# A hybrid layer's first stage: an earlier conditioning block, and two query units accumulated pair by pair

## The chip, the cores and the metric

The kernel runs on one core of a Trainium2 chip. The metric is the device time of one execution in microseconds (us), as the median of several runs. The engines are named as in the profile: PE is TensorE (PEld its weight loads), DVE is VectorE, ACT is ScalarE, POOL is GpSimd, and SP is SyncE, which here issues nearly all DMAs. TensorE's clock is granted at one of two levels, 1.2 and 2.4 GHz; the profile writes the granted share of the higher one.

## The reference

One layer of a diffusion backbone over 1024 tokens of width 1024, with 256 context tokens in front. What matters here is its beginning:

```python
mod = (jax.nn.silu(c) @ ada_w + ada_b)[:, None, :]
sh1, sc1, g1, sh2, sc2, g2 = jnp.split(mod, 6, axis=-1)
h = modulate(rms_norm(x, norm1_w), sh1, sc1)      # h * (1 + scale) + shift
p = h @ w_in                                      # queries, keys, values, z, and the SSD inputs
```

Neighbourhood attention and a bidirectional state-space scan then run on `p`, and an output projection, a second modulated norm and a gated MLP follow; a final norm ends the layer. All data are float32, and the products are computed from a high and a low part of each operand.

## The kernel before

Features lie on the 128 partitions. x is held as 8 feature tiles (`kt` 0 to 7) by 1024 tokens, in two halves of 512 tokens (`h` 0 and 1). A product of float32 accuracy is three matmuls: `hh` times `wh`, `hl` times `wh`, `hh` times `wl`, where `hh` and `hl` are the high and low part of the normalised input and `wh` and `wl` those of a weight block (`load_w`, L72 to L80, splits a loaded block `ws` on ACT and DVE). `mm3` (L82 to L89) runs these three over the feature tiles; a matmul takes 512 columns, so that 1024 tokens need two.

The conditioning (`ada`, L155 to L170) is done in eight blocks of 1 MB for the part that the first norm needs. Blocks 0 to 3 give the shift, blocks 4 to 7 the scale, two feature tiles each. A block is loaded into one of four buffers (`adaw`), multiplied on PE in 16 matmuls (`adap`), copied by ACT (`adas`), folded on PE (`mp`, 4 matmuls), and DVE adds the bias (`mod`, `modc`). The PSUM pool `m1p`, which `adap`, `mp` and the statistics share, has two slots.

The first stage (L129 to L200) loads x, forms for each half the sum of squares (`sq_x`, `sqa_x`), turns it by PE into a row of reciprocal roots (`stat_x`, `rst_x`, `dg_x`, and the broadcast `rbt`), and then goes over four pairs of feature tiles: blocks 4 + i and i of the conditioning, then for both halves and both tiles of the pair DVE's `ny`, ACT's `hh` and DVE's `hl` (`norm`, L172 to L176). Three weight blocks for the first query and key units are loaded on the way (`pre`). The PSUM pool `mmp` has three slots of 1024 columns: the broadcast rows hold one until the last `ny`, the query units take the others. The second stage (from L228) uses the memory that the first stage's pools have given back: it loads tables, the context tokens and 32 rows of the later conditioning (`adal`, L203 to L208), multiplies the two query and two key groups (`fu_qk`, 48 matmuls per unit), rotates them on DVE and stores them, and then computes the values (`tu_v`).

The order of the instructions on each engine and of the loads on SP is not the order of the program text. A planner simulates the program and lets each engine take, of what is ready by the simulated time, what stands first in the text; it also places the semaphore waits. On the chip every engine then keeps the planned order.

Of the kernel before, what the change touches and what calls it, by code (L numbers as in the profile page):

```python
# [10 lines left out]
FP = mybir.dt.float32  # L11
# [6 lines left out]
P = 128  # L18
T = 1024
TC = 256  # L20
KT = 8
# [15 lines left out]
def hymba(ctx: ExitStack, tc: tile.TileContext, A):  # L37
# [35 lines left out]
    def load_w(src, nk, nf, name):  # L73
        n = nk * nf
        s, h, l = (w_tile(tag, f"{tag}_{name}") for tag in ("ws", "wh", "wl"))
        sp.dma_start(s[:, :n], src)
        act.activation(h[:, :n], s[:, :n], AF.Copy)  # L77
        dve.tensor_tensor(l[:, :n], s[:, :n], f32(h[:, :n]), OP.subtract)
        pat = "p (k f) -> p k f"
        return h[:, :n].rearrange(pat, k=nk), l[:, :n].rearrange(pat, k=nk)  # L80
# [22 lines left out]
            pe.matmul(rb[:, t * P:e * P], ones, dg[:, t:e], start=True, stop=True)  # L103
        return rb

    # ---------------------------------------------------------------- projections
    pa = ExitStack()
    hx = pa.enter_context(tc.tile_pool(name="hx", reuse_waits="tile", bufs=1))
    pc = ExitStack()
# [8 lines left out]
    pre = {}  # L118

    with ExitStack() as p0:  # L120
        adap = p0.enter_context(tc.tile_pool(name="adap", reuse_waits="tile", bufs=4))
        xin = p0.enter_context(tc.tile_pool(name="xin", reuse_waits="tile", bufs=1))
        wk0 = p0.enter_context(tc.tile_pool(name="wk0", reuse_waits="tile", bufs=2))

        cc = wk0.tile([P, KT, 2], FP, name="cc", bufs=1)
        sc = hx.tile([P, KT, 32], FP, name="sc")
        sel = wk0.tile([P, 2], FP, name="sel", bufs=1)
        xt = xin.tile([P, KT, T], FP, name="xt")
        sp.dma_start(cc, A["cc"])  # L129
        xh = [xt[:, :, 512 * h:512 * h + 512] for h in range(2)]  # L130

        def load_x(h):
            for kt in range(0, KT, 2):
                sp.dma_start(xh[h][:, kt:kt + 2], A["xt"][:, kt:kt + 2, 512 * h:512 * h + 512])

        load_x(0)
        sp.dma_start(sel, A["sel"])
        sp.dma_start(vec, A["vec"])
        sp.dma_start(cst, A["cst"])
        dve.memset(sc, 0.0)  # L140
        act.activation(sc[:, :, 0:2], cc, AF.Silu)

        def stats(wk0, src, n, key):
            st = m1p.tile([P, 8], FP, tag="m1", name=f"stat_{key}")
            acc = wk0.tile([P, n * P], FP, tag=f"sqa{n}", name=f"sqa_{key}", bufs=1)
            for kt in range(KT):
                sq = acc if kt == 0 else wk0.tile([P, n * P], FP, tag=f"ny{n}", name=f"sq_{key}{kt}", bufs=n)
                act.activation(sq, src[:, kt], AF.Square)
                if kt:
                    dve.tensor_tensor(acc, acc, sq, OP.add)  # L150
            for t in range(n):
                pe.matmul(st[:, t:t + 1], acc[:, t * P:(t + 1) * P], ones1, start=True, stop=True)
            return st[:, :n]

        def ada(b):  # L155
            w = adap.tile([P, KT, 256], FP, tag="ada", name=f"adaw{b}")
            sp.dma_start(w, A["ada_w"][b])
            pr = m1p.tile([P, 256], FP, tag="m1", name=f"adap{b}")
            for kt in range(KT):
                j = kt % 4  # L160
                pe.matmul(pr[32 * j:32 * j + 32], sc[:, kt], w[:, kt], start=kt < 4, stop=kt >= 4,
                          skip_group_check=True)
            sb = wk0.tile([P, 256], FP, tag="adas", name=f"adas{b}")
            act.activation(sb, pr, AF.Copy)
            mp = m1p.tile([P, 2, 2], FP, tag="m1", name=f"mp{b}")
            for f in range(2):
                pe.matmul(mp[:, f], sb[:, f * P:(f + 1) * P], sel, start=True, stop=True)
            c0 = 2 * b
            for m_, col in ((mod, 0), (modc, 1)):
                dve.tensor_tensor(m_[:, c0:c0 + 2], mp[:, :, col], vec[:, V_AB + c0:V_AB + c0 + 2], OP.add)  # L170

        def norm(src, rb, a, b, oh, ol, kt, n, key):  # L172
            y = wk0.tile([P, n], FP, tag=f"ny{n // P}", name=f"ny_{key}{kt}", bufs=n // P)
            dve.scalar_tensor_tensor(y, src[:, kt], a, rb, OP.mult, OP.mult)
            act.activation(oh[:, kt], y, AF.Identity, bias=b)
            dve.scalar_tensor_tensor(ol[:, kt], y, b, f32(oh[:, kt]), OP.add, OP.subtract)  # L176

        rbt = mmp.tile([P, T], FP, tag="mm", name="rbt")
        rbx = [rbt[:, 512 * h:512 * h + 512] for h in range(2)]
        rstd_rows(mmp, wk0, stats(wk0, xh[0], 4, "x0"), 4, "mm", "x0", "sqa4", rb=rbx[0])  # L180
        for i in range(4):
            ada(4 + i)
            if i == 0:
                load_x(1)
            ada(i)
            if i < 3:
                pre[i] = load_w(A["wf"][8 + i], KT, P, f"qk0{i}")
            s2 = slice(2 * i, 2 * i + 2)
            for j, m_ in enumerate((mod, modc)):
                dve.scalar_tensor_tensor(scl[:, j, s2], m_[:, 8 + 2 * i:10 + 2 * i], 1.0,  # L190
                                         vec[:, V_N1 + 2 * i:V_N1 + 2 * i + 2], OP.add, OP.mult)
            for h in range(2):
                if i == 0 and h:
                    rstd_rows(mmp, wk0, stats(wk0, xh[1], 4, "x1"), 4, "mm", "x1", "sqa4", rb=rbx[1])
                for kt in (2 * i, 2 * i + 1):
                    c = slice(512 * h, 512 * h + 512)
                    norm(xh[h], rbx[h], scl[:, 0, kt:kt + 1], mod[:, kt:kt + 1], hh[:, :, c], hl[:, :, c], kt, 512, f"x{h}")

    hs = (hh, hl)
    cs = (ch, cl)  # L200
# [28 lines left out]
    with ExitStack() as p1:  # L229
# [40 lines left out]
        for blk in range(4):  # L270
            if blk == 2:
                context()
            isq = blk < 2
            g = blk % 2
            pq = []
            if not isq:
                oc = wk.tile([P, 2, 2, TC], FR, tag="oc", name=f"oc{blk}", bufs=1)
            for f2 in range(2):
                wt = pre[2 * blk + f2] if 2 * blk + f2 in pre else load_w(A["wf"][8 + 2 * blk + f2], KT, P, f"qk{blk}{f2}")
                if not isq:  # L280
                    ps = fm_unit(wt, cs, TC, m1p, "m1", f"kc{blk}{f2}")
                    split_to(oc, f2, ps, False)
                pq.append(fm_unit(wt, hs, T, mmp, "mm", f"qk{blk}{f2}"))
            if not isq:
                store_heads(oc, k_d, g, T, TC)
            pA, pB = pq
            s = 0.125 if isq else 1.0
            o = wk.tile([P, 2, 2, T], FR, tag="qko", name=f"qko{blk}", bufs=1)
            for comp, (c1, c2, o2) in enumerate(((0, 1, OP.subtract), (1, 0, OP.add))):
                t1 = wk.tile([P, T], FP, tag="rp1", name=f"rp1_{blk}{comp}", bufs=2)  # L290
                t2 = wk.tile([P, T], FP, tag="rp2", name=f"rp2_{blk}{comp}", bufs=1)
                dve.scalar_tensor_tensor(t1, pA, s, cossin[:, c1], OP.mult, OP.mult)
                dve.scalar_tensor_tensor(t2, pB, s, cossin[:, c2], OP.mult, OP.mult)
                dve.tensor_tensor(t1, t1, t2, o2)
                split_to(o, comp, t1, isq)
            store_heads(o, q_d if isq else k_d, g, 0, T)
# [26 lines left out]
    sd = ExitStack()  # L323
    ssd = sd.enter_context(tc.tile_pool(name="ssd", reuse_waits="tile", bufs=1, side="right"))
    dtp = sd.enter_context(tc.tile_pool(name="dtp", reuse_waits="tile", bufs=1, side="right"))
    # dt, decays and cumulative sums, tokens on partitions
    dtv = dtp.tile([P, 10, 16], FP, name="dtv")
    dta = dtp.tile([P, 10, 16], FP, name="dta")
    dtt = ExitStack()
# [239 lines left out]

    pa.close()  # L570

    # ---------------------------------------------------------------- attention and SSD
    pb = ExitStack()
    at = pb.enter_context(tc.tile_pool(name="at", reuse_waits="tile", bufs=2))
    bigp = pb.enter_context(tc.tile_pool(name="bigp", reuse_waits="tile", bufs=3, space=PSUM))
# [194 lines left out]
        pass  # L770
    pb.close()

    # ---------------------------------------------------------------- output projection, second half
    psp = ctx.enter_context(tc.tile_pool(name="psp", reuse_waits="tile", bufs=8, space=PSUM))

    def bank(name, n=512):
# [19 lines left out]
            for o, i in ((4, 0), (4, 2), (5, 0), (5, 2), (6, 0), (6, 2), (3, 2))]  # L796
    yzf = yz.rearrange("p a b -> p (a b)")

    # the gated MLP's first product in seven block products of half the size (Strassen)
    ORDER = ((0, 4), (1, 1), (2, 2), (3, 0), (4, 3), (5, 0), (6, 3))  # L800

    B_SUMS = (((0, 0),), ((1, 0), (0, 0), OP.subtract), ((1, 1),), ((0, 0), (1, 1), OP.add),
# [123 lines left out]
    b_ops(0, (5, 6))  # L926
    second = norm2(1, range(7))

    # ---------------------------------------------------------------- gated MLP
    def g_load(hf_, k):  # L930
        h, l = gslots[k - 8]
        sp.dma_start(f32(l), g_d[k, :, 512 * hf_:512 * hf_ + 512])
# [34 lines left out]
    g_load(0, 20)  # L967
    g_load(0, 21)

    # ---------------------------------------------------------------- down projection and final norm  # L970
    # of its 22 blocks along the sum, 8 go by the same seven block products and 14 directly
    mt4 = yz[:, 4:6].rearrange("p a (b t) -> p (a b) t", b=2)
    m1, m4, m5, m45 = (mt4[:, i] for i in range(4))
    srow = [yz[:, 6], ssum[1]]
# [186 lines left out]
```

## Time and profile before

| | us |
|---|---|
| median of 3 runs | 1435.97 |
| lowest and highest run | 1433.61, 1436.22 |
| span of the profiled execution | 1432.0 |
| PE busy in it | 1344.9 |
| DVE busy in it | 955.2 |
| ACT busy in it | 598.9 |
| POOL busy in it | 583.6 |

The profiled execution's own time is shown only as its span, from its first to its last instruction; the runs' times have what lies around the span as well. Busy times are shares of one execution over stages with different limits. A row of the timeline gives the start in us, the length, engine, line, operation, output and inputs, and how many like instructions it joins; in brackets the idle time of the engine just before it and what ended that.

### The profile page before, as it was taken

The numbers are of one execution on the slowest core, as the hardware profiler recorded it, in microseconds if no ns is written. First come the engines' busy times: TensorE is split into PE (matmuls) and PEld (weight loads), VectorE is DVE, ScalarE is ACT, GpSimd is POOL, SyncE is SP. The second block draws the span as 40 slices with busy tenths as digits, with TensorE's granted clock in tenths as the row PEclk, the third lists the DMA queues.
The fourth block names the chain that finished last, engine by engine and source line by source line (L and its number), as shares of the span: only waits on it lengthen the run. The fifth ranks groups of instructions, "written<-read, shape, count | busy, mean of one in ns | idle before, by whom it ended". The sixth has DMA issues, their size and how long they took to land.

```text
span 1432.0 us, 19634 instructions
## 1 busy us (share of the span) xinstructions
PE 1344.9 (94%) x7539; PEld 1126.8 (79%) x7539; DVE 955.2 (67%) x1251; ACT 598.9 (42%) x987; POOL 583.6 (41%) x389
## 2 busy tenths in 40 slices
PE   5999899999989998999889999999999989998996
PEld 3788888889868787778777777777778767887885
DVE  5797434232367766548989777777787796488574
ACT  5432124342155558535535333344343443354331
POOL 0020000013657852014565676666676554334250
PEclk8999999999989999999989999999999999999998
DMA  9578862021697787343213222212222464364342
GB/s 372 213 238 233 245 228 77 30 74 38 181 253 204 208 222 256 100 153 111 74 48 115 74 89 74 60 73 88 89 88 89 134 224 140 107 199 125 107 141 74
DMA packets 86909, 202.23 MB, mean 141 GB/s; under 512 B 8472, under 2 KB 33816, under 8 KB 85536
## 3 DMA queue, kind: packets, MB, share of 16 engines
q1 hardware_dynamic: 83648, 189.45, 42.3%
q0 software_dynamic: 3168, 11.54, 2.0%
q8 instruction: 59, 0.97, 0.3%
q14 instruction: 34, 0.28, 0.1%
HBM read 163.40 MB, written 37.55 MB: 140 GB/s over the span
## 4 chain that ended last, share of the span: by engine, by line
PE 65%; DVE 15%; DMA 8%; issue 4%; ACT 3%; POOL 3%; SPq 2%; DVEq 0%; ACTq 0%; POOLq 0%
PE u L856 23%; PE pd L88 8%; PE fu_x L88 6%; PE pm L1010 3%; PE av L655 2%; PE tu_z L88 2%; PE oc L88 2%; PE tu_v L88 2%; DMA adal<-in_ada_wt 2%; PE os L88 2%; DMA seg<-cum_d 2%; PE pt L637 2%; PE oa L88 2%; PE s L616 1%; DVE wlu L849 1%
## 5 line engine op out<-in xcount | busy, mean ns | idle before, releaser
L856 PE MATMUL u<-op,whu 128*128 128x512 f32 (+1 forms) x760 | 229.7, 386 | 5.9 <-ACT whu L848 2.5
L856 PEld LDWEIGHTS u<-op,whu 128*128 128x128 f32 x760 | 141.9, 192 | 38.0 <-ACT whu L848 2.7
L856 PE MATMUL u<-op,wlu 128*128 128x512 f32 (+1 forms) x380 | 145.9, 385 | 2.2 <-DVE wlu L849 2.2
L849 DVE TENSOR_TENSOR wlu<-yz,whu 128x512 fp32r<-128x512 f32 x115 | 135.9, 1196 | 17.5 <-ACT whu L848 16.8
L847 POOL TENSOR_TENSOR yz<-as,as 128x512 f32<-128x512 f32 x69 | 118.9, 1735 | 46.7 <-DVE wlu L849 45.8
L848 ACT ACTIVATE whu<-yz 128x512 fp32r<-128x512 f32 x115 | 70.9, 626 | 116.1 <-PE u L856 68.0
L856 PE MATMUL u<-opx,whu 128*128 128x512 f32 (+1 forms) x384 | 113.1, 383 | 3.5 <-ACT whu L848 3.5
L395 POOL TENSOR_TENSOR xwc<-ctm,wendc 128x512 f32<-128x512 f32 x4 | 4.7, 1166 | 218.6 <-PE fu_c L88 200.9
L847 POOL TENSOR_TENSOR yz<-as 128x512 f32<-128x512 f32 x46 | 64.0, 1400 | 62.1 <-DVE wlu L849 52.4
L856 PEld LDWEIGHTS u<-opx,whu 128*128 128x128 f32 x384 | 69.6, 191 | 22.2 <-ACT whu L848 8.9
L856 PEld LDWEIGHTS u<-op,wlu 128*128 128x128 f32 x380 | 73.0, 192 | 17.6 <-DVE wlu L849 2.6
L88 PE MATMUL pd<-opx,wh_dn 128*128 128x512 f32 x256 | 80.6, 398 | 3.7 <-ACT wh_dn L77 3.7
L856 PE MATMUL u<-opx,wlu 128*128 128x512 f32 (+1 forms) x192 | 72.7, 380 | 0.0
L887 POOL TENSOR_TENSOR xa<-xa 128x1024 f32<-128x1024 f32 x20 | 51.7, 2586 | 45.6 <-DVE xa L877 45.4
L628 ACT ACTIVATE pr<-pr,mx 128x640 f32<-128x640 f32 x64 | 52.8, 826 | 40.5 <-DVE mx L627 40.4
L627 DVE CUSTOM_DVE_ANT_0 pr<-s,tabt 128x640 f32<-128x640 f32 x64 | 52.0, 818 | 20.6 <-PE s L617 15.8
L849 DVE TENSOR_TENSOR wlu<-as,whu 128x512 fp32r<-128x512 f32 x46 | 46.2, 1004 | 26.0 <-ACT whu L848 26.0
L655 PE MATMUL av<-pts,vp 128*64 128x128 f32 x640 | 56.4, 289 | 5.5 <-ACT pts L639 4.9
L208 DVE CUSTOM_DVE_ANT_0 adal<-adal,crow 128x1024 f32<-128x1024 f32 x32 | 39.6, 1240 | 30.8 <-DMA adal<-in_ada_wt 30.8
L88 PEld LDWEIGHTS pd<-opx,wh_dn 128*128 128x128 f32 x256 | 47.5, 188 | 16.0 <-ACT wh_dn L77 4.8
L856 PE MATMUL u<-opz,whu 128*128 128x512 f32 (+1 forms) x192 | 57.4, 381 | 0.6 <-DVE opz L816 0.6
L639 ACT ACTIVATE pts<-pt 128x640 f32<-128x640 f32 x64 | 43.8, 696 | 32.2 <-PE pt L637 20.3
(660 smaller groups left out, 3785.5 us busy)
## 6 DMA issues: line engine op xcount, KB each, us to landing
as<-in_w_up SPq DMA_DIRECT2D x46, 512.0 KB, 4.2
adal<-in_ada_wt SPq DMA_DIRECT2D x32, 512.0 KB, 4.7
ws_dn<-in_w_down SPq DMA_DIRECT2D x32, 448.0 KB, 3.5
g_d<-xa POOLq DMA_DIRECT2D x22, 512.0 KB, 4.5
tabt<-in_tab SPq DMA_DIRECT2D x48, 192.0 KB, 4.4
adaw<-in_ada_w SPq DMA_DIRECT2D x8, 1024.0 KB, 12.2
seg<-cum_d SPq DMA_DIRECT2D x16, 512.0 KB, 5.5
q<-q_d SPq DMA_DIRECT2D x32, 256.0 KB, 6.5
```

The costliest lines, as they stand in the source:

```text
L88: pe.matmul(out[:, t0:t1], st(a, k), mv(b, k, t0, t1), start=k == 0 and p == 0, stop=k == kend - 1 and p == 2, **kw)
L208: dve.tensor_tensor_reduce(w, w, crow, 1.0, 0.0, OP.mult, OP.add, modr[:, f - 16:f - 15])
L627: dve.tensor_tensor_reduce(pr, ps[:, lo:lo + 640], tabt[m % 2][:, 384 * j:384 * j + 640], -1.0, BIG, OP.add, OP.min, mx)
L628: act.activation(pr, pr, AF.Exp, bias=mx, scale=-1.0, accum_out=sm[:, n % 8:n % 8 + 1])
L639: act.activation(pts, pt[:, 0:640], AF.Copy)
L655: pe.matmul(av[64 * j:64 * j + 64, cb], vt, pp[j][:, i * P:(i + 1) * P], start=i == 0, stop=i == 4, skip_group_check=True)
L847: pool.tensor_tensor(src, e[0], e[1], e[2])
L848: act.activation(h, src, AF.Copy)
L849: dve.tensor_tensor(l, src, f32(h), OP.subtract)
L856: pe.matmul(ps[:, t0:t1], aops[n, o][a][:, k], bops[o][b][:, k, t0:t1], start=first and o < 5 and (t0 == 0 or n == 2), stop=end, skip_grou ...
L887: (dve if p == 0 else pool).tensor_tensor(r[i], r[i], tmp, OP.mult)
L1010: pe.matmul(dst[o], aops[n, o][a][:, k], sops[o][b][:, k], start=k == i == 0 and (o in (0, 2, 4) or o > 4 and first), stop=k == 3 and i == ...
```

## The change

The load of a conditioning block is taken out of `ada` into `ada_load`, and its place in the text changes: block 4 is requested right behind the first half of x and ahead of `vec` and `cst`, block 0 behind these and ahead of the second half of x. Blocks 5 and 1, 6 and 2, 7 and 3 are requested one turn of the loop ahead, before the weight block of the next turn. Two accumulators for the first two query units (`early`) are taken at the start, and a new function `early_mm` multiplies one unit, one half and a pair of feature tiles as soon as the loop has normalised them; unit 1 takes the first two pairs together in the second turn. In the second stage the first group uses these accumulators in place of `fm_unit`. The statistics of the first half of x now stand in the text behind the first two conditioning blocks and the first weight block. Some comment lines were removed.

```diff
+        adaw = {}
+
+        def ada_load(b):
+            adaw[b] = adap.tile([P, KT, 256], FP, tag="ada", name=f"adaw{b}")
+            sp.dma_start(adaw[b], A["ada_w"][b])
+
         load_x(0)
         sp.dma_start(sel, A["sel"])
+        ada_load(4)
         sp.dma_start(vec, A["vec"])
         sp.dma_start(cst, A["cst"])
+        ada_load(0)
+        load_x(1)
...
         def ada(b):
-            w = adap.tile([P, KT, 256], FP, tag="ada", name=f"adaw{b}")
-            sp.dma_start(w, A["ada_w"][b])
+            w = adaw.pop(b)
...
-        rstd_rows(mmp, wk0, stats(wk0, xh[0], 4, "x0"), 4, "mm", "x0", "sqa4", rb=rbx[0])
+        early = [mmp.tile([P, T], FP, tag="mm", name=f"fu_qk0{u}") for u in range(2)]
+
+        def early_mm(u, h, kts):
+            wt = pre[u]
+            for k in kts:
+                for p, (a, b) in enumerate(((0, 0), (0, 1), (1, 0))):
+                    pe.matmul(early[u][:, 512 * h:512 * h + 512], wt[a][:, k], (hh, hl)[b][:, k, 512 * h:512 * h + 512],
+                              start=k == 0 and p == 0, stop=k == KT - 1 and p == 2)
+
         for i in range(4):
-            ada(4 + i)
+            for b in (4 + i, i):
+                ada(b)
             if i == 0:
-                load_x(1)
-            ada(i)
+                pre[0] = load_w(A["wf"][8], KT, P, "qk00")
+                rstd_rows(mmp, wk0, stats(wk0, xh[0], 4, "x0"), 4, "mm", "x0", "sqa4", rb=rbx[0])
             if i < 3:
+                ada_load(5 + i)
+                ada_load(1 + i)
+            if i in (1, 2):
                 pre[i] = load_w(A["wf"][8 + i], KT, P, f"qk0{i}")
...
+            kts = (2 * i, 2 * i + 1)
             for h in range(2):
                 if i == 0 and h:
                     rstd_rows(mmp, wk0, stats(wk0, xh[1], 4, "x1"), 4, "mm", "x1", "sqa4", rb=rbx[1])
-                for kt in (2 * i, 2 * i + 1):
+                for kt in kts:
                     c = slice(512 * h, 512 * h + 512)
                     norm(xh[h], rbx[h], scl[:, 0, kt:kt + 1], mod[:, kt:kt + 1], hh[:, :, c], hl[:, :, c], kt, 512, f"x{h}")
+                early_mm(0, h, kts)
+                if i:
+                    early_mm(1, h, (0, 1, 2, 3) if i == 1 else kts)
...
-                pq.append(fm_unit(wt, hs, T, mmp, "mm", f"qk{blk}{f2}"))
+                pq.append(early[f2] if blk == 0 else fm_unit(wt, hs, T, mmp, "mm", f"qk{blk}{f2}"))
```

## Rows read from the trace of the kernel before

**Rows 1.** The page's first line.
```profile
span 1432.0 us, 19634 instructions
```

**Rows 2.** Windows: stretch, length, busy time per engine (instructions), granted clock, DMA share, GB/s.
```profile
20.00:45.00 25.00, 21.84 (x139) 14.51 (x140) 21.58 (x42) 13.20 (x22) 0.00 (x0) 0.73 1.02 415
26.10:34.40 8.30, 8.29 (x48) 4.91 (x48) 5.49 (x12) 4.59 (x7) 0.00 (x0) 0.53 1.01 408
34.40:57.80 23.40, 23.40 (x160) 17.59 (x157) 16.70 (x37) 7.57 (x14) 0.00 (x0) 1.00 0.61 242
46.00:53.00 7.00, 7.00 (x58) 4.79 (x56) 3.85 (x11) 2.84 (x5) 0.00 (x0) 1.00 0.02 8
57.80:153.40 95.60, 95.60 (x505) 81.74 (x506) 72.39 (x103) 31.20 (x54) 8.24 (x8) 1.00 0.79 235
153.40:186.00 32.60, 23.47 (x179) 22.86 (x178) 19.59 (x32) 6.92 (x9) 0.00 (x0) 0.90 0.84 250
```

**Rows 3.** Chain of waits, first 60 us: start, length, what.
```profile
26.11 1.84 PE stat_x L152 x8
27.95 1.86 PE adap L161 x16
...
29.81 0.73 PE fu_qk L88
...
34.43 1.38 PE fu_qk L88 x5
...
37.15 4.38 PE fu_qk L88 x18
...
42.87 5.09 PE fu_qk L88 x21
...
49.30 2.44 PE fu_qk L88 x9
...
53.08 4.36 PE fu_qk L88 x18
57.44 0.35 PE mp L167 x4
```

**Rows 4.** Chain of waits from 60 to 215 us.
```profile
174.60 8.69 DMA adal<-in_ada_wt
...
185.88 26.25 PE tu_v L88 x214
```

**Rows 5.** Timeline of what the change touches; SPq rows are DMA issues.
```profile
5.35 4.24 SPq L134 DMA_DIRECT2D xt<-in_xt  x4
...
10.62 2.77 SPq L157 DMA_DIRECT2D adaw<-in_ada_w  x2
...
21.07 1.94 PE L161 MATMUL adap<-adaw,sc 128*32 128x256 f32 x16 [3.40 <-DMA adaw<-in_ada_w]
...
23.06 1.04 ACT L77 ACTIVATE wh_qk<-ws_qk 128x1024 fp32r<-128x1024 f32 x1
24.01 0.61 ACT L148 ACTIVATE sq_x<-xt 128x512 f32<-128x512 f32 x1
...
26.19 1.33 ACT L175 ACTIVATE hh<-ny_x,mod 128x512 fp32r<-128x512 f32 x2 [1.30 <-DVE mod L170]
...
34.50 0.33 SPq L157 DMA_DIRECT2D adaw<-in_ada_w  x1
...
52.50 2.72 DVE L174 SCALAR_TENSOR_TENSOR ny_x<-xt,scl,rbt 128x512 f32<-128x512 f32 x4
...
53.20 0.39 ACT L164 ACTIVATE adas<-adap 128x256 f32<-128x256 f32 x1 [1.84 <-PE adap L161]
...
58.01 2.58 ACT L175 ACTIVATE hh<-ny_x,mod 128x512 fp32r<-128x512 f32 x4 [4.42 <-DVE mod L170]
...
60.21 8.39 SPq L207 DMA_DIRECT2D adal<-in_ada_wt  x4
```

**Rows 6.** Landing times of the conditioning blocks' loads, from issue.
```profile
DMA to landing us min/median/max: 8.2/12.2/14.1
```

## The prediction

> **What bounds the kernel now.** I read the page for the span [rows 1], then the windows over the front of the kernel, then the chain of waits through the same stretch, and last the timeline around what the change moves. The whole edit lies in the first 60 us of 1432.0. In the windows the reader is to see three different limits in a row [rows 2]. From 20 to 45 us the DMA engines are full (share 1.02, 415 GB/s). From 26.1 to 34.4 us TensorE has no gap (8.29 of 8.30 us) but its granted clock is 0.53, the lower of its two levels, 1.2 GHz; from 34.4 to 57.8 us it again has no gap (23.40 of 23.40), now at 2.4 GHz. From 46 to 53 us the DMA engines do nothing (0.02). From 57.8 to 153.4 us TensorE is full, and from there to 186 us it stands idle for 32.60 - 23.47 = 9.1 us.
>
> The chain of waits says which of these sets the end [rows 3]. From 26.11 us it runs on TensorE without a break up to the last conditioning product, `mp` at 57.44 us. In between lie the matmuls of six of the eight conditioning blocks, the first of them at 27.95, and six pieces of the query product `fu_qk`: 1 + 5 + 18 + 21 + 9 + 18 = 72 matmuls. A pair of feature tiles is 12 matmuls for one query unit and 24 for two, so 72 is exactly the first three of the four pairs, for both units. So the kernel before accumulates the two query units pair by pair already: the planner has pulled `fu_qk` forward as filler. After 60 us the chain is no longer on TensorE but on VectorE and on transfers such as `adal` [rows 4], and the first of these loads is issued at 60.21 us, while the last four `hh` from 58.01 us on come to their end [rows 5]: its buffers lie where those of the norms lay. So the end of the first stage counts twice: as TensorE's work and as the start of the later loads.
>
> **The change part by part.**
>
> *Loads.* No byte is added: eight 1 MB blocks, x and the weights are the same. The first shift block (`adaw0`) goes ahead of the four loads of the second half of x, `adaw4` ahead of `vec` and `cst`. Now the matmul on `adaw0` waits 3.40 us for its transfer and starts at 21.07 us [rows 5]; the half of x is 2.1 MB, at 415 GB/s 5.1 us. So `adaw0` would land at about 16.0. The work ahead of it on TensorE ends at 21.07 - 3.40 = 17.7 us, so it would start there, 3.4 us earlier. The first `hh` starts at 26.19 now [rows 5]; with its matmul 3.4 us earlier, and the copy no longer behind the square of the second half that starts at 24.01, I put it at 21.5 us. What it costs: the second half of x lands 1 MB later, 2.5 us. The last of its loads is issued by 9.6 us, and the last square on it starts only at 24.01 [rows 5]; VectorE's running sum sets that, not the transfer. I count nothing. With that cover gone it would cost up to 2.5 us. `vec` and `cst` come 2.5 us later and are not wanted before the first statistics are done; nothing again.
>
> *What TensorE does with it.* `adaw5` does not come earlier: the same bytes are ahead of it. It is issued at 10.62 and the longest landing of these blocks is 14.1 us, so 24.7 us [rows 5, 6]. The statistics of the second half of x stand at 26.11 us in the chain, `adaw5`'s matmuls at 27.95 [rows 3]. In the new order they could swap, and TensorE's unbroken work would begin at 24.7 instead of 26.1: 1.4 us. Bounds: -1.7 (the two `hl` of the first pair, 1.4 us, and two small ones go ahead of VectorE's running sum and delay the statistics) to +3.0 (it starts with the split of the first weights at 23.06 [rows 5]). I take 1.4, nearest to the row of the load.
>
> *Accumulation of the first half before the second.* The six matmuls of unit 0, pair 0, first half need `hh` (21.5) and the split weights (`wh` starts at 23.06 and takes 1.04 us). Four of the six need no low weight part and can run in the hole before 26.1; now only one of the six runs before 34.43 [rows 3]. At the pace 4.38 / 18 = 0.243 us that takes 4 x 0.243 = 1.0 us out of the later full stretch. Bounds 0 (none fits) and 1.2 (five more). I take 1.0.
>
> *Clock.* The rise from 1.2 to 2.4 GHz comes at the end of the unbroken 8.3 us of rows 2. Moved with it, it costs nothing more. If it stays where it is, 1.4 us of work is done at half speed and 0.7 us is lost; if the four matmuls in the hole bring it forward by another 1.5 us, 0.7 us is won. I take 0.4.
>
> *Order of the conditioning chain.* The later blocks are requested ahead of the second and third weight block. Now `adaw3` is issued at 34.50 us, and with the longest landing of 14.1 us it is there by 48.6, while its matmuls stand right ahead of the piece at 53.08; so TensorE's order limits, not the transfer. Each query matmul that the planner puts behind the last `mp` instead of ahead of it ends the stage 0.243 us earlier. Bounds: 0, and a whole pair, 24 x 0.243 = 5.8 us, above. The nearest row is the piece of 9 matmuls among those of 18 and 21, which shows that the filler between two blocks varies by about 10. Nothing says that a shorter filler is the rule, so I take 4 matmuls, 1.0 us.
>
> *Passing on.* The sum is 1.4 + 1.0 + 0.4 + 1.0 = 3.8 us at the end of the first stage. From 60 to 186 us the chain lies on VectorE and on transfers that start with the buffers freed there, so it moves along; TensorE's 9.1 us of idle time behind 153.4 us say that TensorE alone would not pass it on. Bounds 0 and 3.8; I take all of it, because the DMA engines stand still from 46 to 53 us just for want of those buffers. What is late next is then the same stretch of `adal` loads, only earlier. A new plan can also reorder the later stages; the 9.1 us of that hole, half of them either way, is the nearest row for what that can do.
>
> The profiled execution has a span of 1432.0 us; the runs are 1433.6 to 1436.2, median 1435.97, so some 4.0 us lie around the span. 1432.0 - 3.8 = 1428.2, with 4.0 around it **1432.2 us**.
>
> **The rivals.**
>
> *Conditioning runs ahead.* If the planner lets the last two blocks go before the third pair's 24 matmuls, the stage ends 5.8 us earlier on top of 1.4 + 1.0 + 0.4: 8.6 us, 1427.4. For it: `adaw3` lies unused for over 4 us now. Against: that freedom was there before and was not used.
>
> *Absorbed.* TensorE gains but the stretch from 60 to 186 us, whose DMA share is high and whose chain ends in an 8.69 us wait for `adal` [rows 4], ends where it did, or the half clock eats it: a gain of at most 1 us, 1435.5. For it: the change's second part does what the planner already did. Against: those loads cannot be issued before the norms are done.
>
> *Order in force, slower.* The new calls stand ahead of the next pair's conditioning in the program. If the planner keeps them there, TensorE takes a pair's 24 matmuls first, then both blocks, and then stands until the next `hh` exists: copy 0.39, `mp` 0.35, `ny` 2.72 / 4 = 0.68, `hh` 2.58 / 4 = 0.65 [rows 3, 5], 2.07 us at each of three borders, 6.2 us. Less the 2.8 us of the first three terms that is 3.4 slower, 1439.4. It decides from 0.9 us of idle time at a border. For it: no third unit can fill the gap, because its accumulator is the one the broadcast rows hold until the last `ny`. Against: where nothing is ready the planner fills, as rows 3 show. The Trainium skill speaks for this rival: in TensorE: Matmul & The Clock Gate, Part 3 (The mechanism), matmuls start and end in strict program order. By that rule one early matmul waiting for its norm holds up the conditioning blocks behind it; the trace agrees in so far as `mp` follows the 18 matmuls ahead of it. The same page, under Why this matters for your kernels, warns against idle gaps between bursts of matmuls, because the clock falls back; the 0.53 from 26.1 us on, behind the 3.40 us of waiting at 21.07, agrees, and this rival would become dearer by it.
>
> **How the numbers follow.** Forecast 0.42, with a range of its own of 1430 to 1434.5; conditioning ahead 0.18; absorbed 0.20; slower 0.20. About 0.2%, 2.9 us, is what a measurement can tell from no change, that is below 1433.1 or above 1438.8. The forecast gives 0.30 to faster and 0.12 to no change, the rival ahead 0.18 to faster; the absorbed case 0.17 to no change and 0.03 to slower; the last rival 0.17 to slower and 0.03 to no change. Faster 0.48, same 0.32, slower 0.20. The range 1427 to 1440 leaves out the far ends of the two outer cases.
>
> **What would show it.** Right: the first `hh` near 21.5 us instead of 26.19; TensorE unbroken from about 24.7; `fu_qk` before 26 us; the last `mp` near 53.6 us; the first `adal` issued near 56.4; `tu_v`'s long run near 182 instead of 185.88. Wrong: a last `mp` later than 57.4, gaps of TensorE before `hh` between pairs, a clock of 0.5 after 34 us, or a first `adal` that is earlier and a `tu_v` run that is not.

## The result, and the profile after

The changed kernel takes 1445.51 us (median of 4 runs, 1443.41 to 1446.55), the kernel before 1434.90 us beside it (4 runs). The ratio is 1.0078, with an interval of 1.0057 to 1.0099: some 11 us slower. The forecast was 1432.2 us and faster, the range 1427 to 1440; the time lies above all of it.

The page's first line for the changed kernel answers to [rows 1]; the profiled execution is 12.1 us longer.

```profile
span 1444.1 us, 19625 instructions
```

The windows of the changed kernel answer to [rows 2], over the same stretches or those that took their place (stretch, length, busy time and instructions of PE, PEld, DVE, ACT and POOL, granted clock, DMA share, GB/s).

```profile
20.00:45.00 25.00, 19.02 (x90) 10.82 (x91) 17.39 (x29) 11.11 (x19) 0.00 (x0) 1.00 0.94 371
26.80:38.50 11.70, 9.99 (x37) 5.95 (x37) 8.44 (x12) 5.45 (x9) 0.00 (x0) 1.00 0.95 385
38.50:71.80 33.30, 30.82 (x187) 20.62 (x187) 17.76 (x40) 8.47 (x16) 0.00 (x0) 1.00 0.36 134
46.00:53.00 7.00, 6.31 (x27) 4.66 (x28) 3.50 (x9) 2.69 (x5) 0.00 (x0) 1.00 0.35 140
71.80:168.00 96.20, 93.75 (x484) 78.94 (x484) 73.14 (x104) 31.07 (x54) 8.56 (x8) 0.98 0.78 233
```

TensorE had no gap from 26.1 to 57.8 us before [rows 2]; now it stands for 1.7 of 11.7 us and for 2.5 of 33.3 us, and between 46 and 53 us it runs 27 matmuls where it ran 58. The stage's last `mp`, at 57.28 us in the timeline before (the chain's piece in [rows 3] has 57.44), is at 71.38.

The timeline of the changed kernel shows where that begins (start, length, engine, line, operation, how many; in brackets the idle time of the engine ahead of it and what ended that).

```profile
6.59 5.51 DVE L159 TENSOR_TENSOR sqa_x<-sqa_x,sq_x 128x512 f32<-128x512 f32 x7 [5.39 <-ACT sq_x L157]
12.15 1.93 PE L169 MATMUL adap<-adaw,sc 128*32 128x256 f32 x16 [12.15 <-DMA adaw<-in_ada_w]
15.89 1.93 PE L169 MATMUL adap<-adaw,sc 128*32 128x256 f32 x16 [0.30 <-DMA adaw<-in_ada_w]
18.32 1.01 PE L175 MATMUL mp<-sel,adas 128*128 128x2 f32 x4 [0.49 <-ACT adas L172]
19.19 1.84 PE L161 MATMUL stat_x<-ones,sqa_x 128*128 128x1 f32 x8
21.07 0.26 ACT L93 ACTIVATE rst_x<-stat_x,epst 128x4 f32<-128x4 f32 x1 [1.51 <-PE stat_x L161]
22.39 2.07 PE L103 MATMUL rbt<-dg_x,cst 128*128 128x512 f32 x2 [1.35 <-DVE dg_x L99]
24.50 0.63 ACT L157 ACTIVATE sqa_x<-xt 128x512 f32<-128x512 f32 x1 [0.96 <-PE rbt L103]
26.07 1.32 ACT L183 ACTIVATE hh<-ny_x,mod 128x512 fp32r<-128x512 f32 x2
26.84 0.79 PE L194 MATMUL fu_qk<-hh,wh_qk 128*128 128x512 f32 x1 [2.37 <-ACT hh L183]
34.88 1.70 PE L161 MATMUL stat_x<-ones,sqa_x 128*128 128x1 f32 x8
36.51 1.93 PE L169 MATMUL adap<-adaw,sc 128*32 128x256 f32 x16
71.38 0.50 PE L175 MATMUL mp<-sel,adas 128*128 128x2 f32 x4
73.69 2.28 SPq L231 DMA_DIRECT2D adal<-in_ada_wt  x2
```

The same steps in the kernel before, from its timeline:

```profile
11.88 1.87 PE L152 MATMUL stat_x<-ones,sqa_x 128*128 128x1 f32 x8 [11.88 <-DVE sqa_x L150]
13.68 1.93 PE L161 MATMUL adap<-adaw,sc 128*32 128x256 f32 x16
15.55 1.79 PE L103 MATMUL rbt<-dg_x,cst 128*128 128x512 f32 x2
17.37 0.63 ACT L148 ACTIVATE sqa_x<-xt 128x512 f32<-128x512 f32 x1 [1.30 <-PE rbt L103]
27.88 1.93 PE L161 MATMUL adap<-adaw,sc 128*32 128x256 f32 x16
57.28 0.50 PE L167 MATMUL mp<-sel,adas 128*128 128x2 f32 x4
57.64 0.71 PE L88 MATMUL fu_qk<-hh,wh_qk 128*128 128x512 f32 x2
```

Read the two downward together. VectorE has the first half's sum of squares ready at 6.59 + 5.51 = 12.10 us, 0.2 us later than before. But TensorE's planned order now has two whole conditioning blocks ahead of the eight small matmuls `stat_x`: they run at 19.19 instead of 11.88 us. The roots, the broadcast `rbt` (22.39 against 15.55) and, behind these on ScalarE, the first square of the second half (24.50 against 17.37) move along by the same 7 us. The second half's `stat_x` comes at 34.88 against 26.11 us [rows 3], and the fifth block's `adap`, the next in TensorE's order, at 36.51 against 27.88. The block for it had been requested from 12.42 us on, only 1.8 us later than before [rows 5].

### The profile page after: what moved, and what is told of

Its sections match the earlier page's. It is cut to its first block, busy times and chain, and to the rows that moved or that the text cites. A ratio compares the mean times of both kernels' runs of the same rounds, so it can differ in the third digit from the quotient of the medians.

```text
span 1444.1 us, 19625 instructions
## 1 busy us (share of the span) xinstructions
PE 1347.0 (93%) x7539; PEld 1123.8 (78%) x7539; DVE 961.9 (67%) x1251; ACT 597.7 (41%) x987; POOL 580.5 (40%) x389
## 4 chain that ended last, share of the span: by engine, by line
PE 44%; DVE 11%; issue 3%; ACT 3%; DMA 2%; POOL 1%; DVEq 0%; SPq 0%; ACTq 0%; POOLq 0%
PE u L880 23%; PE pd L88 8%; PE pm L1034 3%; PE os L88 2%; PE oa L88 2%; PE oc L88 1%; DVE op L1015 1%; PE pd L1034 1%; DVE wlu L873 1%; PE av L679 1%; DVE op L840 1%; PE pt L661 1%; DMA xa<-g_d 1%; DVE bst L1011 1%; DVE xa L917 1%
## 5 line engine op out<-in xcount | busy, mean ns | idle before, releaser
L872 ACT ACTIVATE whu<-yz 128x512 fp32r<-128x512 f32 x115 | 70.9, 626 | 114.8 <-PE u L880 65.8
L88 PE MATMUL pd<-opx,wh_dn 128*128 128x512 f32 x256 | 80.6, 398 | 2.9 <-ACT wh_dn L77 2.9
L88 PEld LDWEIGHTS pd<-opx,wh_dn 128*128 128x128 f32 x256 | 47.5, 188 | 15.1 <-ACT wh_dn L77 4.0
L679 PE MATMUL av<-pts,vp 128*64 128x128 f32 x640 | 54.4, 281 | 4.4 <-ACT pts L663 3.8
L661 PE MATMUL pt<-cst,pr 128*128 128x128 f32 x320 | 49.1, 285 | 8.8 <-ACT pr L652 4.4
```

Of the source, the lines that this page charges most:

```text
L88: pe.matmul(out[:, t0:t1], st(a, k), mv(b, k, t0, t1), start=k == 0 and p == 0, stop=k == kend - 1 and p == 2, **kw)
L661: pe.transpose(pt[:, i * P:(i + 1) * P], pr[:, i * P:(i + 1) * P], ident)
L679: pe.matmul(av[64 * j:64 * j + 64, cb], vt, pp[j][:, i * P:(i + 1) * P], start=i == 0, stop=i == 4, skip_group_check=True)
L872: act.activation(h, src, AF.Copy)
```

## The experiments

The change has three parts that can be undone by themselves: L, the loads' places; E, the two units' matmuls inside the loop (`early`); S, the statistics of the first half, moved in the text behind the first two blocks. The theory was that S is what costs; the rivals were E (the new matmuls in TensorE's order), L (the second half of x landing later) and the shared buffer `sqa4`. The table holds all runs. Its columns are the start of the second `stat_x`, of the last `mp` and of the first `adal` load, the query matmuls (`fu_qk`) that the trace has up to 72 us, the start of the last `tu_v` matmul (the end of the values), all of the profiled execution, and the ratio to the kernel before. Some matmul records can be missing.

| kernel | `stat_x` 2 | last `mp` | `adal` | `fu_qk` by 72 | `tu_v` ends | ratio (interval) |
|---|---|---|---|---|---|---|
| before | 26.1 | 57.3 | 60.2 | 134 | 211.8 | 1 |
| e2, L | 26.8 | 56.8 | 60.4 | 136 | 210.0 | 1.0005 (0.9992 to 1.0018) |
| e3, E | 26.9 | 58.2 | 62.1 | 118 | 216.1 | 1.0035 (1.0021 to 1.0049) |
| e1, L and E | 27.0 | 58.1 | 62.7 | 118 | 216.7 | 1.0019 (1.0000 to 1.0037) |
| e4, S | 40.1 | 71.7 | 74.0 | 72 | 225.6 | 1.0083 (1.0056 to 1.0109) |
| e5, S and L | 33.8 | 64.4 | 66.7 | 103 | 217.3 | 1.0036 (1.0017 to 1.0055) |
| after, all | 34.9 | 71.4 | 73.7 | 93 | 227.5 | 1.0078 (1.0057 to 1.0099) |
| e6, all, own buffer | 34.6 | 71.1 | 73.5 | 94 | 227.0 | one run |
| e7, both statistics early | 21.5 | 56.0 | 59.6 | 139 | 209.7 | 0.9982 (0.9964 to 0.9999) |
| e8, both ahead of the loop, with L | 24.0 | 62.2 | 65.8 | 113 | 213.8 | 1.0032 (1.0013 to 1.0050) |
| e9, fewer queries ahead | 26.8 | 50.5 | 53.5 | 125 | 213.3 | 1.0009 (0.9992 to 1.0027) |
| e10, e7 with that | 21.6 | 50.7 | 54.4 | 124 | 215.8 | 1.0029 (1.0013 to 1.0045) |
| e11, e7 with part of that | 21.8 | 57.1 | 60.7 | 129 | 209.3 | 0.9981 (0.9961 to 1.0000) |

**Statistics put back.** The changed kernel with one line moved back.

```diff
+        rstd_rows(mmp, wk0, stats(wk0, xh[0], 4, "x0"), 4, "mm", "x0", "sqa4", rb=rbx[0])
         for i in range(4):
...
                 pre[0] = load_w(A["wf"][8], KT, P, "qk00")
-                rstd_rows(mmp, wk0, stats(wk0, xh[0], 4, "x0"), 4, "mm", "x0", "sqa4", rb=rbx[0])
```

> The changed kernel with one line put back: the statistics of the first half of x stand in the text ahead of the conditioning loop, as before; early loads and early accumulation stay. Theory A (the late statistics are the loss: stat_x of the first half on TensorE at 19.2 instead of 11.9 us): stat_x at 11.9, the second half's statistics back from 34.9 to 26 to 28 us, and 1432 to 1436 us, about 10 less than the changed kernel's 1445.5. Theory B (the early matmuls hold up the conditioning blocks behind them): stat_x at 11.9 but fifth block and last mp still late, 1442 to 1446. Theory C (the second half of x lands too late): 1443 to 1446.

Measured: 1435.36 us, ratio 1.0019. TensorE's rows in its timeline are those of the kernel before again, within a microsecond:

```profile
11.94 1.87 PE L161 MATMUL stat_x<-ones,sqa_x 128*128 128x1 f32 x8 [11.94 <-DVE sqa_x L159]
27.02 1.70 PE L161 MATMUL stat_x<-ones,sqa_x 128*128 128x1 f32 x8
28.65 1.93 PE L169 MATMUL adap<-adaw,sc 128*32 128x256 f32 x16
```

With loads and early matmuls left in, moving this line takes the loss from 11.2 us (0.0078 of 1434.9) to 2.7.

**Loads alone.** The kernel above without `early` and `early_mm`.

```diff
-                early_mm(0, h, kts)
-                if i:
-                    early_mm(1, h, (0, 1, 2, 3) if i == 1 else kts)
...
-                pq.append(early[f2] if blk == 0 else fm_unit(wt, hs, T, mmp, "mm", f"qk{blk}{f2}"))
+                pq.append(fm_unit(wt, hs, T, mmp, "mm", f"qk{blk}{f2}"))
```

> Early loads alone: statistics first and the two query units by fm_unit as before. Theories A and B: no loss; the first conditioning chain starts 3 us earlier, and 1431 to 1435 us, at or somewhat below the kernel before (1434.9). Theory C: the loss stays, 1443 to 1446.

Measured: 1434.75 us, ratio 1.0005: no change. From its timeline:

```profile
22.10 1.32 ACT L183 ACTIVATE hh<-ny_x,mod 128x512 fp32r<-128x512 f32 x2
```

and in the same view, on TensorE:

```profile
26.79 1.84 PE L161 MATMUL stat_x<-ones,sqa_x 128*128 128x1 f32 x8
```

The first `hh` does come 4.1 us earlier than in [rows 5], near the forecast 21.5. But the second half's statistics come no earlier: VectorE's running sum for them ends at 26.64 us, with the first pair's two `hl` (23.04 to 24.45 us) now ahead of its last three additions. That is the delay which the prediction's lower bound priced. TensorE's unbroken work still waits for them.

**Early matmuls alone.** The same with E and without L.

```diff
-        ada_load(4)
...
-        ada_load(0)
-        load_x(1)
...
         def ada(b):
+            ada_load(b)
             w = adaw.pop(b)
...
+                if b == 4:
+                    load_x(1)
...
-            if i < 3:
-                ada_load(5 + i)
-                ada_load(1 + i)
```

> Early accumulation alone: loads in the order of before, statistics first, early_mm in the loop. Theory A: 1434 to 1437, since the planner already filled with these matmuls. Theory B: 1440 to 1446, with the last mp after 60 us against 57.3 and the first adal load after 63 against 60.2. Theory C: 1434 to 1436.

Measured: 1439.82 us, ratio 1.0035, 5.0 us slower, a little below theory B's range; the last `mp` and the first `adal` come earlier than B said. TensorE does not stand before `hh` here: the new matmuls wait for nothing, and the last `mp`, with 72 query matmuls ahead of it as before, comes only 0.9 us later. The loss lies behind it. The timeline, and a window in the form of [rows 2]:

```profile
57.03 2.72 DVE L180 SCALAR_TENSOR_TENSOR ny_x<-xt,scl,rbt 128x512 f32<-128x512 f32 x4
59.80 1.22 PE L88 MATMUL fu_qk<-hh,wh_qk 128*128 128x512 f32 x2 [1.03 <-DVE ny_x L180]
61.68 1.06 PE L88 MATMUL fu_qk<-hh,wl_qk 128*128 128x512 f32 x2
...
63.79 0.62 PE L88 MATMUL fu_qk<-hh,wl_qk 128*128 128x512 f32 x2
60.00:63.00 3.00, 3.00 (x8) 2.35 (x9) 2.38 (x4) 2.98 (x5) 0.00 (x0) 0.50 0.97 344
```

The third pair's matmuls now stand ahead of the `mp` that the last norms need, so that the last `ny` start at 57.03 instead of 52.50 us [rows 5]. Their broadcast rows hold the accumulator that the third query unit takes. That unit went on at 57.64 us before, straight behind the last `mp`; here it waits for the `ny` and starts at 59.80, and its first eight matmuls run at half pace, at a granted clock of 0.50. From 26 to 72 us TensorE is idle for 1.75 us, 1.6 more than before, and eight matmuls at half pace lose another 1.7. That is 3.3 of the 3.9 us that the 16 missing matmuls make (118 up to 72 us instead of 134). `adal` comes 1.9 us later. The run with the loads left in (e1) shows the same wait and the same half pace from 60 us on.

**Late statistics alone.** The kernel before with the one line moved.

```diff
-        rstd_rows(mmp, wk0, stats(wk0, xh[0], 4, "x0"), 4, "mm", "x0", "sqa4", rb=rbx[0])
         for i in range(4):
...
                 pre[i] = load_w(A["wf"][8 + i], KT, P, f"qk0{i}")
+            if i == 0:
+                rstd_rows(mmp, wk0, stats(wk0, xh[0], 4, "x0"), 4, "mm", "x0", "sqa4", rb=rbx[0])
```

> The kernel before with one line moved: the statistics of the first half of x stand behind the first two conditioning blocks and the first weight block. With the old order of loads block 0 lands only at about 21 us, so TensorE would reach these statistics at 25 us. Theory A: a loss of at least the changed kernel's, 1443 to 1450, the second half's statistics at 35 us or later. Theory B and C: 1434 to 1437.

Measured: 1445.79 us, ratio 1.0083: the whole loss of the change with one of its lines. The timeline shows the chain, later still than in the changed kernel, because the second block (`adaw0`) is not requested early here:

```profile
21.20 1.93 PE L161 MATMUL adap<-adaw,sc 128*32 128x256 f32 x16 [4.48 <-DMA adaw<-in_ada_w]
24.61 1.85 PE L152 MATMUL stat_x<-ones,sqa_x 128*128 128x1 f32 x8
40.06 1.83 PE L152 MATMUL stat_x<-ones,sqa_x 128*128 128x1 f32 x8 [6.58 <-DVE sqa_x L150]
```

**Late statistics with the loads, no early matmuls.** The changed kernel without `early`, the same edit as in "Loads alone".

> The changed kernel without the early accumulation: loads early, statistics of the first half of x behind the two conditioning blocks, query units by fm_unit. If late statistics alone carry the loss (7.3 us on TensorE's first statistics): 1440 to 1442, the first adal load at 67 to 68 us against 60.2 before and 73.7 in the changed kernel, and the early matmuls cost the rest of the changed kernel, 4 us. If the early accumulation adds nothing once the statistics are late: 1444 to 1446 and the first adal load at 73.

Measured: 1439.36 us, ratio 1.0036, 5.2 us slower. Its timeline:

```profile
19.24 1.85 PE L161 MATMUL stat_x<-ones,sqa_x 128*128 128x1 f32 x8
33.75 1.84 PE L161 MATMUL stat_x<-ones,sqa_x 128*128 128x1 f32 x8 [1.81 <-DVE sqa_x L159]
```

The early load earns something after all where the statistics wait behind the block that it brings: `stat_x` at 19.24 instead of 24.61 us, and of the 11.9 us of the run before 6.7 come back. Putting the early matmuls in again then costs 11.2 - 5.2 = 6.0 us. So the change adds up along this path as +11.9 (S), -6.7 (L), +6.0 (E), and along the other as +0.7 (L), +2.0 (E), +8.5 (S). The first term of each path carries the uncertainty of one interval (3.8 us for S, 1.9 for L); each difference behind it carries 3 to 5 us from its two intervals, so that the +2.0 of E can't be told from nothing. The parts are not additive, and neither S nor E is the whole loss once L is in; S is the larger on both paths, on the first only just beyond the uncertainty.

**The buffer that the two halves share.** `dg_x` of the first half and the running sum of the second lie in one buffer, `sqa4`. The row at 24.50 us waits for the broadcast that reads it.

```diff
-rstd_rows(mmp, wk0, stats(wk0, xh[0], 4, "x0"), 4, "mm", "x0", "sqa4", rb=rbx[0])
+rstd_rows(mmp, wk0, stats(wk0, xh[0], 4, "x0"), 4, "mm", "x0", "dga4", rb=rbx[0])
```

(and so for the second half).

> The changed kernel with a buffer of its own for the broadcast's diagonal dg, so that the second half's running sum sqa no longer shares a slot with it and need not wait for the first broadcast. If the slot hands the delay of the first statistics on to the second: the second half's stat_x at 30 us or earlier instead of 34.9, the first adal load 4 us earlier, 1439 to 1442. If the order of the queues hands it on (on ACT the squares stand behind the root of the first half, on VectorE the sums behind the first two ny): stat_x of the second half within 1 us of 34.9, 1443 to 1446.

Measured: 1449.79 us in one run, so only the trace is read. ScalarE:

```profile
20.95 0.26 ACT L93 ACTIVATE rst_x<-stat_x,epst 128x4 f32<-128x4 f32 x1 [1.51 <-PE stat_x L161]
21.11 0.62 ACT L157 ACTIVATE sqa_x<-xt 128x512 f32<-128x512 f32 x1
22.35 1.06 ACT L77 ACTIVATE wh_qk<-ws_qk 128x1024 fp32r<-128x1024 f32 x1 [0.62 <-DMA ws_qk<-in_wf]
23.31 1.13 ACT L157 ACTIVATE sq_x<-xt 128x512 f32<-128x512 f32 x2
25.35 1.38 ACT L183 ACTIVATE hh<-ny_x,mod 128x512 fp32r<-128x512 f32 x2 [0.91 <-DVE ny_x L182]
26.64 3.13 ACT L157 ACTIVATE sq_x<-xt 128x512 f32<-128x512 f32 x5
```

The first square comes 3.4 us earlier, yet the second `stat_x` only 0.3 (34.56). The buffer's wait was real but not last: the first square still stands behind the root `rst_x` in ScalarE's order, and the rest behind the first weight split (`wh_qk`) and `hh`. So the buffer does not explain the late second `stat_x`.

**Both statistics early.** If late statistics cost, earlier ones than before should gain. The kernel before, with the second half's statistics moved up, right behind the request of their data, and with the separate buffer for `dg_x`.

```diff
                 load_x(1)
+                rstd_rows(mmp, wk0, stats(wk0, xh[1], 4, "x1"), 4, "mm", "x1", "dga4", rb=rbx[1])
             ada(i)
...
-                if i == 0 and h:
-                    rstd_rows(mmp, wk0, stats(wk0, xh[1], 4, "x1"), 4, "mm", "x1", "sqa4", rb=rbx[1])
```

> The kernel before with the second half's statistics moved forward in the text, right behind that half's load, and a buffer of its own for dg. Theory A in the other direction (the second half's statistics gate TensorE's unbroken work): its stat_x at 20 to 21 us instead of 26.1, the first adal load at 55 to 57 instead of 60.2, and 1429 to 1432 us. If the conditioning chain or its loads gate the stage instead: first adal load at 59 to 61 and 1433 to 1436.

Measured: 1431.33 us, ratio 0.9982, 2.6 us faster, with an interval that ends at 0.9999.

```profile
14.51 0.63 ACT L148 ACTIVATE sqa_x<-xt 128x512 f32<-128x512 f32 x1 [0.42 <-DMA xt<-in_xt]
```

```profile
21.47 1.84 PE L152 MATMUL stat_x<-ones,sqa_x 128*128 128x1 f32 x8 [3.76 <-DVE sqa_x L150]
```

ScalarE's first square now waits for the load alone and the statistics come 4.6 us earlier. Only a part arrives: the first `adal` is 0.6 us earlier, less than was expected (55 to 57 us; it is at 59.6), and the first `hh`, now behind these squares, is at 30.0 us instead of 26.19 [rows 5]. The run makes two edits at once, and which of them earns the gain was not separated.

**Both statistics ahead of the loop, with the early loads.** The kernel of "Loads alone" with both statistics ahead of the loop and the separate buffer. In the run before, the second statistics stood behind the first conditioning block (`ada(4)`); here they stand ahead of it.

> Early loads as in the change, no early accumulation, and the statistics of both halves of x in the text ahead of the conditioning, with a buffer of its own for dg. The second half of x lands at 20.9 us here, so its stat_x comes at 22 to 23. Theory A: first adal load at 57 to 59, 1430 to 1434 us, behind the previous kernel because the first conditioning block waits on TensorE for these statistics. If conditioning gates: 1434 to 1437.

Measured: 1439.51 us, ratio 1.0032, slower, and above both of the ranges expected.

```profile
23.99 1.86 PE L161 MATMUL stat_x<-ones,sqa_x 128*128 128x1 f32 x8 [6.57 <-DVE sqa_x L159]
25.78 1.93 PE L169 MATMUL adap<-adaw,sc 128*32 128x256 f32 x16
```

Here TensorE stands 6.57 us for the statistics while the first two blocks, which in the changed kernel had landed by 12.15 and 15.89 us, lie behind them. In this order the early loads of those blocks are of no use. How much of the loss is the loads' and how much the place of the statistics ahead of the first block was not separated.

**Fewer query matmuls ahead of the last block.** This tests the step that was to pass a gain on, though not by itself: TensorE also gets less done ahead of the last block. In the kernel before, a third accumulator is held until the norms are done, so that only one unit can run as filler. It adds one small VectorE instruction at each end.

```diff
         rbt = mmp.tile([P, T], FP, tag="mm", name="rbt")
+        held = mmp.tile([P, T], FP, tag="mm", name="held")
+        heldc = hx.tile([P, 1], FP, name="heldc")
+        dve.memset(held[:, 0:1], 0.0)
...
+            if i == 3:
+                dve.tensor_tensor(heldc, mod[:, 2 * i + 1:2 * i + 2], held[:, 0:1], OP.add)
```

> The kernel before with the third accumulator slot held by an empty tile until the last pair's conditioning is there, so that only one query unit can fill TensorE in the first stage: 36 query matmuls stand ahead of the last mp instead of 72. By the pace of 0.243 us per matmul the last mp comes up to 8.7 us earlier, bounded by the last block's landing at 44 us: first adal load at 52 to 54 us against 60.2. If the end of the first stage, that is the loads into its freed buffers, sets what follows: 1427 to 1430 us. If TensorE's own amount of work up to 150 us sets it, the idle time put in is not won back: 1434 to 1440 us.

Measured: 1435.44 us, ratio 1.0009: no change. The last `mp` on TensorE:

```profile
50.45 0.50 PE L167 MATMUL mp<-sel,adas 128*128 128x2 f32 x4
```

and the `adal` loads, from SP's view (lengths in ns, first and last issue in us):

```profile
L212 SPq DMA_DIRECT2D adal<-in_ada_wt x32: 327/328/2335, 53.5 to 169.5; - x32
```

The stage ends 6.8 us earlier with half the filler (36 query matmuls ahead of the last `mp`), and the loads begin 6.7 us earlier. Nothing of it reaches the end: `tu_v` ends 1.5 us later, with 9 query matmuls fewer done by 72 us.

**The hold on top of both statistics early**, in full (until the last norms) and in part (`if i == 2`, until those of the third pair).

> Both halves' statistics first (as in the run that came out at 1431.3) and the held slot together. If the stage's end sets what follows: first adal load at 50 to 53 us, 1424 to 1428 us. If TensorE's amount of work sets it: 1431 to 1437 us.

> The same with the slot held only until the third pair's conditioning is there: the second unit fills in behind it, 66 query matmuls stand ahead of the last mp. Between the two: if the stage's end sets it, first adal load at 56 to 59 us and 1428 to 1431 us; if TensorE's amount of work sets it, 1430 to 1433 us, no worse than without the held slot.

Measured: 1437.06 us, ratio 1.0029, for the full hold, and 1430.65 us, ratio 0.9981, for the part. The full hold turns the gain of both statistics early into a loss although its `adal` begins 5.2 us ahead of that kernel's. The partial one keeps the gain and adds nothing that can be measured; its `adal` is at 60.7 us, not at the 56 to 59 expected, and its time lies in both ranges, so it decides nothing between them. These two, both statistics early with and without the partial hold, are the fastest kernels here: some 3 us below the kernel before, at the edge of what the runs can tell, and by their ratios 14 below the changed one.

## Why the prediction was wrong

**The step that failed is "TensorE's unbroken work would begin at 24.7 instead of 26.1: 1.4 us", with bounds of -1.7 to +3.0.** The second half's statistics came at 34.88 us, 8.8 us later than before and far outside the bounds. The bounds priced delays of VectorE's sum by neighbours. They didn't price the move of the first half's statistics behind two blocks, which the document ahead of the prediction lists as a part of the change and the prediction's account never takes up. The step on the loads assumed it away in one number: "the work ahead of it on TensorE ends at 21.07 - 3.40 = 17.7 us" counts `stat_x` and `rbt` as done by then, but in the new order they stand behind `adaw0`'s matmuls. Where each engine is given first what stands first in the text, the place of that line was a term of its own. Late statistics alone measured 1.0083, with the early loads beside them 1.0036, the whole change 1.0078; the change without the late statistics 1.0019.

**Loads.** `adaw0` was forecast to land at about 16.0 us, and its matmuls start on its landing at 15.89. The first `hh` was forecast at 21.5 us: it is at 22.1 in the kernels with the loads and the statistics in their old place, and at 26.07 in the changed one. "I count nothing" for the later second half of x held: its statistics are at 26.8 with the loads alone, 0.7 later. In the run with the loads alone the earlier `hh` is worth nothing that can be measured (1.0005): the second half's statistics, ahead of TensorE's unbroken work, came no earlier.

**Four matmuls in the hole and the clock, 1.4 us together.** Four query matmuls were forecast ahead of the second `stat_x`; twelve ran there, with the fifth conditioning block pushed back behind them and the statistics. They came at half pace. In the timeline of the changed kernel:

```profile
28.64 0.63 PE L194 MATMUL fu_qk<-hh,wh_qk 128*128 128x512 f32 x1
29.07 0.63 PE L194 MATMUL fu_qk<-hl,wh_qk 128*128 128x512 f32 x1
...
42.78 0.39 PE L194 MATMUL fu_qk<-hh,wl_qk 128*128 128x512 f32 x1
43.01 0.39 PE L194 MATMUL fu_qk<-hh,wh_qk 128*128 128x512 f32 x1
```

0.43 us from start to start near 29 us, 0.23 near 43. Twelve times the difference is 2.4 us.

**Order of the conditioning chain.** Four matmuls fewer were forecast ahead of the last `mp`; there are 92 in place of 72. The 72 of the first two units stand ahead of the last block in the text and are done when its `adap` ends; between that and its `mp` the planner puts 20 of the third unit (L88, from 66.61 us), where before 18 of the first two filled [rows 3]. 20 times 0.243 us is 4.9 us. Between the changed kernel and the one without early matmuls (72) the last `mp` differs by 71.4 - 64.4 = 7.0 us; the later second `stat_x` gives 1.1 of that.

**The rival "order in force"** (1439.4 us) had the sign of the early matmuls and nearly their size: it gave 3.4 us slower with all else going right; early matmuls alone measured 5.0, and 6.0 on top of the other two parts. Its mechanism was another. The 6.2 us of idle time at the borders between pairs are not there. From 20 to 80 us the new matmuls of the changed kernel (L194) wait for `hh` three times, 3.9 us in all (total, times, longest):

```profile
PE fu_qk L194 <- ACT hh L183: 3.9, 3, 2.4
```

2.37 of the 3.9 us is the first wait, at 26.84, ahead of any border; the other two are 0.26 and 1.23. With the statistics in their old place the new matmuls do not wait for `hh` at all (with the loads left in there is one wait of 5.0 us for the first split weights, but without the new matmuls it is there too, at 5.4). The order did cost, one step later: the last norms, the third unit's accumulator and the half pace that followed ("Early matmuls alone"). The Trainium skill's rule that the rival cited, that matmuls start and end in program order (TensorE: Matmul & The Clock Gate, Part 3, The mechanism), agrees with the trace where it mattered most: `stat_x` had its input at 12.10 us and ran at 19.19, straight behind the `mp` at 18.32.

**"Passing on"** took 60 to 186 us to follow the first `adal`. Delays do pass: 13.5 us at `adal` became 15.7 at the end of `tu_v`. An earlier `adal` alone did not pass: with the hold it was 6.7 us early for nothing, but the hold also left query matmuls undone, so it does not show that no gain can pass. The table fits a later-of-two reading. Put the shift of `adal` beside the missing query matmuls times 0.243 us: late statistics 13.8 and 15.1, `tu_v` 13.8 later; statistics and loads 6.5 and 7.5, 5.5 later; early matmuls 1.9 and 3.9, 4.3 later; the hold -6.7 and 2.2, 1.5 later; the changed kernel 13.5 and 10.0, 15.7 later. The later of the two is right within 4 us in all twelve kernels. Alone, the missing matmuls miss by 5.7 us in the changed kernel and 5.5 in its copy with the own buffer and are within 4 elsewhere, and the shift of `adal` misses by 8.2 and 9.8 us in the two full holds. That is read off the runs and not shown: both statistics early with the loads (5.6 and 5.1, but 2.0 later) and with the partial hold (0.5 and 1.2, but 2.5 earlier) lie farthest off, and which wait of the rotations and tables carries it was not isolated. TensorE's largest wait in `tu_v` is for VectorE's `rp`, 6.4 us before, 8.1 after, 7.6 with the hold. Past `tu_v` the changed kernel gets 15.7 - 12.1 = 3.6 us back by its end. The delay is still 15.6 us at the last `tu_z` matmul (398.3 against 382.7 us) and 10.0 at the last `oc` matmul (706.2 against 696.2); why it shrinks between them stays open.

**The other signs named.** The last `mp` later than 57.4 us, named as a sign of a wrong prediction, is there; of gaps before `hh` between pairs there are the two small ones. A granted clock of 0.5 behind 34 us isn't shown in the changed kernel's windows; see the last section.

**The base of the sum.** The 4.0 us put around the span compares the span of one execution with the median of others. Of one execution, the changed kernel's profiled one, the time is 1445.83 us and the span 1444.1, so 1.7 lie around it. The forecast does not hang on it: it is the median less 3.8.

## What to carry to other kernels

Price every line that a diff moves, above all a short chain that many later steps need: eight tiny matmuls moved behind two 1 MB blocks cost, moved alone, as much as the whole change. Where an engine keeps a planned order, ask of each moved group what now stands ahead of it on every engine that it passes, and follow the delay to the next thing that waits. Here an earlier load (1.0005) and a stage that ended earlier with less work done in it (1.0009) earned nothing; before counting such a gain, test whether what ends last behind it was waiting for it.

## What the runs showed of the hardware

The granted clock in the windows could not be taken at its word at the start of these traces. For the changed kernel it reads 1.00 in every window up to 84 us, yet the 16 matmuls of one conditioning block take 1.93 us at 36.51 and 1.07 us in this row at 40.28:

```profile
40.28 1.07 PE L169 MATMUL adap<-adaw,sc 128*32 128x256 f32 x16
```

In the kernel before they take 1.93 us at 27.88, in a stretch for which the column gives 0.53 [rows 2]. So TensorE was still at the lower level, 1.2 GHz, at 36.51 us and at the higher one at 40.28; the durations show it and the column does not. The rise came at 34.4 us before [rows 2], so it is some 4 to 6 us later here, and that belongs to the price of the late statistics.

The same holds for the kernel before: its column reads 1.00 up to 20 us, but the 16 matmuls at 13.68 us already take 1.93. So the 0.53 from 26.1 us on, which the prediction read beside the 3.40 us of waiting at 21.07, does not show that the clock fell in that wait; by the durations it had not yet risen. A fall is shown where the early matmuls stand without late statistics. Alone (e3), TensorE stood 0.56 us ahead of the four small `mp` matmuls at 58.16 us and 1.03 us behind them; the granted clock is 1.00 up to 59 us and 0.50 from 60 to 63, two matmuls of 512 columns take 0.85 us from start to start there, and 0.46 from 63.79 on.
